# Forming sums of up-projection weight blocks earlier, in the attention, and passing them through DRAM

## The chip, the cores and the metric

One core of a Trainium2 chip runs the whole program. The metric is the device time of one execution in microseconds; several executions are timed and their median is given. One further execution was taken with the hardware profiler, and every row below is from it. PE is TensorE (matmuls), PEld its weight loads, DVE is VectorE, ACT is ScalarE, POOL is GpSimd and SP is SyncE, which issues the transfers.

## The reference

One encoder layer with shared weights runs on two batches, one of 1024 tokens (`x_prompt`) and one of 512 (`x_sample`), width 1024, all in float32. The layer is

```
h    = rmsnorm(x)
proj = h @ w_in                          # q, k, v of two attentions, and two gates
a    = dilated attention, 3 groups of 4 heads, merged by their log-sum-exp
bo   = windowed attention, 8 query heads on 2 key heads, with a sink
x    = x + (sigmoid(g_a) * (a @ w_a_out) + sigmoid(g_b) * (bo @ w_b_out)) @ w_o
u    = dwconv3(rmsnorm(x) @ w_up)        # width 2 * 2816
y    = x + (gelu(u_gate) * u_val) @ w_down
out  = rmsnorm(y)
```

The part that matters here is `rmsnorm(x) @ w_up` for the 1024 tokens.

## The kernel before, in words

Every float32 matrix is split into a rounded high part and the remainder (`hi`, `lo`), and a product is three matmuls (high by high, high by low, low by high). A weight tile is therefore loaded (`raw`), cast on ScalarE (`whi`, line 138) and its remainder formed on GpSimd, or each third time on VectorE (`wlo`, line 141). This is `wload` (lines 124 to 142). Its `raw` tiles come from one pool of three buffers of 128x1024 float32, and the `whi`, `wlo` tiles from a pool of three pairs; both pools serve all of the kernel but the 1024-token request's feed-forward part.

The order of stages is: the 512-token request as a whole, then the 1024-token request's attention, its merge of the branches, its up-projection and its down-projection.

**Attention** (lines 609 to 716). Six dilated steps (three groups, two pairs of heads each) and four steps of windowed attention follow each other. Each step has four units for the 1024 tokens, so there are 40 units, 24 of them dilated. `_Pipe.run` (lines 75 to 95) works through the units of a step: it calls the unit's score steps in turn, lets the transposes and the value products follow some steps later, and in between draws the projections of the next step (`q_pair`, `k_pair`, `v_group`) from a generator, evenly over the step. The weights of a projection are loaded when its generator starts. The v tiles of groups 1 and 2 are stored to DRAM and loaded back in another order. In this stage the compiler's tile layer orders each engine's queue by when it expects instructions to be ready, program order first among those that are.

**Up-projection of the 1024 tokens** (`up_strassen`, from line 1025). It is a Strassen-like scheme: tokens in two halves, the 1024 inputs in two halves, gate and value columns as two halves, in 22 groups of 128 gate and 128 value columns. A group needs seven products instead of eight (`m1` to `m7`, 12 matmuls each). With g0, g1 the upper and lower halves of the gate columns and v0, v1 those of the value columns, the weights of the products are g0 for m1, g1 for m2, s = v0 + v1 for m5, s - g0 for m6, g0 - v0 for m7, v1 for m4 and g1 - (s - g0) for m3. They take four GpSimd instructions of 128x512 a group: three in `sums` (from line 1053) and one when m7 is prepared. The code of `sums`, with `gp` a GpSimd instruction at line 1051:

```
gp(s, v0, v1, ALU.add)
gp(v0, g0, v0, ALU.subtract)
gp(g0, s, g0, ALU.subtract)
```

In the second line v0 becomes g0 - v0, and in the third g0 becomes s - g0; both work in place in the loaded tiles `rraw` (six buffers of 128x1024), and `s` has a pool `rsum` of three. `prepare` runs four products ahead of TensorE and splits each weight block (`ring_split`, lines 1017 to 1023: cast `rhi` on ScalarE, remainder `rlo` on VectorE) into a ring of seven. A group's gate and value columns are loaded whole at m1, 512 KB each, in pieces of 128 columns. `evacuate` adds the products together and, at m3, does the convolution, the gate and a store of the result to DRAM (line 1105).

The scheme starts while the merge still ends: the generator `quads` (lines 913 to 1004) scales and transposes the tokens (`xn`, line 950), and forms sums of token blocks (`ht`, `t2raw`, line 940; `t1lo`, line 933; `b22lo`). There an order written out by hand (`order`) interleaves its steps with the first products of three groups; up to the step "." each queue has program order.

Of the kernel before, what the change touches and what calls it, by code (L numbers as in the profile page):

```python
# [16 lines left out]
F32 = mybir.dt.float32  # L17
# [3 lines left out]
ALU = mybir.AluOpType  # L21
# [3 lines left out]
P = 128  # L25
D = 1024
KT = D // P
HD = 64
AH = 4
D_FF = 2816  # L30
FT = D_FF // P
# [33 lines left out]
class _Pipe:  # L65
# [9 lines left out]
    def run(self, units, gens, steps):  # L75
# [6 lines left out]
        for a_steps, b_steps, c_step in units:  # L82
            left = [len(b_steps)]
            base = self.t
            for need, b in b_steps:
                self.todo_b.append((base + need + 1 + self.lag_b, b, left, c_step))
# [32 lines left out]
class _Layer:  # L119
# [489 lines left out]
    def attention(self, ctx, rows=None, vectors=None):  # L609
# [39 lines left out]

        cur = {}  # L650
# [6 lines left out]
        for g in range(3):  # L657
            stats = self.sm.tile([P, NT, 2, AH], F32, tag="stats", name="stats")
            for jp in range(2):
# [25 lines left out]
                pipe.run(units, gens, steps)  # L685
# [3 lines left out]
        for pair in range(4):  # L689
# [24 lines left out]
            pipe.run(units, gens, steps)  # L714
# [197 lines left out]

    def quads(self, sm, psum, ptag):
# [111 lines left out]
    def up_strassen(self, quads):  # L1025
# [21 lines left out]
        def block(i, name, kh):  # L1047
            return groups[i][name][:, 4 * kh:4 * kh + 4].rearrange("p k c -> p (k c)")

        def gp(out, a, b, op):  # L1050
            nc.gpsimd.tensor_tensor(out=out, in0=a, in1=b, op=op)

        def sums(i):
            g0, v0, v1 = block(i, "g", 0), block(i, "v", 0), block(i, "v", 1)
            groups[i]["s"] = s = self.rsum.tile([P, 512], F32, tag="rsum", name="rsum")
            gp(s, v0, v1, ALU.add)
            gp(v0, g0, v0, ALU.subtract)
            gp(g0, s, g0, ALU.subtract)

        def prepare(i, m):  # L1060
            g = groups[i]
            blk = lambda name, kh: block(i, name, kh)
            if m == "m1":
                for name, col in (("g", i * P), ("v", D_FF + i * P)):
                    g[name] = raw = self.rraw.tile([P, KT, P], F32, tag="rraw", name="rraw")
                    nc.sync.dma_start(raw, W["w_up"][:, col:col + P].rearrange("(k p) c -> p k c", p=P))
            elif m == "m5" and "s" not in g:
                sums(i)
            elif m == "m7":
                gp(blk("g", 1), blk("g", 1), blk("g", 0), ALU.subtract)  # L1070
            src = {"m1": ("g", 0), "m2": ("g", 1), "m6": ("g", 0), "m7": ("v", 0), "m4": ("v", 1), "m3": ("g", 1)}
            g[m] = self.ring_split(g["s"] if m == "m5" else blk(*src[m]))
# [40 lines left out]
        for i in range(2):  # L1113
            prepare(*next(todo))
            sums(i)
# [299 lines left out]
```

## Time and profile before

| what | us |
|---|---|
| median of three executions | 2269.03 (2264.22 to 2269.49) |
| the profiled execution's own time | 2266.72 |
| its span, first to last instruction | 2264.9 |
| PE busy | 2178.8 |
| DVE, ACT, POOL busy | 1283.3, 1014.9, 517.4 |

The own time is what the timer gave for the profiled execution; the span is what its trace covers, 1.8 us less. Busy times of engines overlap, so they don't add up; an engine that is off the chain costs nothing by being idle. In rows, a time at the left is the start in us from the span's start, the next number is the length; in brackets stands how long the engine sat idle before and which instruction or transfer released it. A queue's issues carry a q (SPq). PEclk is the granted TensorE clock, 1.00 being its upper level.

### The profile page before, as it was taken

The page shows a single profiled execution, that of the slowest core. Times are in us where ns is not written, and L with a number is a line of the kernel's source. Part 1 is how long each engine was busy: PE and PEld are TensorE (multiplying, and loading weights), DVE is VectorE, ACT ScalarE, POOL GpSimd, SP SyncE. Part 2 cuts the span into 40 slices and gives each one's busy share as a digit, 9 for nine tenths or more (in the row PEclk, how much of TensorE's full clock was granted, in tenths as well). Part 3 has the DMA queues.
Part 4 walks back from the last instruction along what each step waited for, and adds up shares of the span by engine and source line. Part 5 has one row for each costly group of instructions (what it writes and reads, how often), then busy time and mean ns, then how long its engine had stood idle before and what let it go on. Part 6 is the DMA issues. An engine that isn't in the chain of part 4 may idle for free.

```text
span 2264.9 us, 28400 instructions
## 1 busy us (share of the span) xinstructions
PE 2178.8 (96%) x10627; PEld 1811.3 (80%) x10627; DVE 1283.3 (57%) x2191; ACT 1014.9 (45%) x1874; POOL 517.4 (23%) x296
## 2 busy tenths in 40 slices
PE   7999999899999999999999999999899999999998
PEld 6887777688878888988787788887778888888887
DVE  4547533644464456465586634325888888863534
ACT  5646532533344336565576211124555555543433
POOL 1211144233333411010000132232333333300000
PEclk9999999999999999999999899999999999999999
DMA  5453452323333331413112911113122222264452
GB/s 169 138 171 115 141 162 89 112 85 110 94 112 112 93 98 47 135 58 122 55 50 83 253 45 54 42 45 131 56 75 84 84 82 80 85 212 142 160 170 102
DMA packets 247981, 240.80 MB, mean 106 GB/s; under 512 B 19808, under 2 KB 204848, under 8 KB 247844
## 3 DMA queue, kind: packets, MB, share of 16 engines
q1 hardware_dynamic: 247844, 238.99, 33.9%
q8 instruction: 83, 1.36, 0.2%
q14 instruction: 54, 0.44, 0.1%
HBM read 202.46 MB, written 42.79 MB: 108 GB/s over the span
## 4 chain that ended last, share of the span: by engine, by line
PE 76%; DVE 6%; issue 3%; ACT 2%; DMA 1%; POOL 1%; SPq 0%; DVEq 0%; ACTq 0%; POOLq 0%
PE psuA L1015 10%; PE psuC L1015 5%; PE pacc L835 4%; PE pacc L1175 3%; PE pacc L1174 3%; PE pacc L1176 3%; PE pacc L834 3%; PE pacc L833 3%; PE psu L148 3%; PE psu L147 3%; PE psu L149 3%; PE psg L149 3%; PE psg L148 3%; PE psg L147 3%; PE psuB L1015 2%
## 5 line engine op out<-in xcount | busy, mean ns | idle before, releaser
L141 POOL TENSOR_TENSOR wlo<-raw,whi 128x1024 fp32r<-128x1024 f32 (+1 forms) x117 | 275.1, 2356 | 901.7 <-ACT whi L138 713.2
L138 ACT CAST whi<-raw 128x1024 fp32r<-128x1024 f32 (+1 forms) x178 | 182.4, 1031 | 380.5 <-PE pacc L835 134.8
L847 DVE TENSOR_TENSOR xacc<-xacc,pacc 128x512 f32<-128x512 f32 x240 | 160.5, 686 | 127.7 <-PE pacc L835 127.3
L141 DVE TENSOR_TENSOR wlo<-raw,whi 128x1024 fp32r<-128x1024 f32 (+1 forms) x61 | 75.7, 1242 | 147.1 <-ACT whi L138 147.0
L147 PE MATMUL psg<-hhi,whi 128*128 128x512 f32 x384 | 149.6, 390 | 1.2 <-ACT frow L520 1.2
L149 PE MATMUL psg<-hhi,wlo 128*128 128x512 f32 x384 | 149.4, 389 | 0.0
L148 PE MATMUL psg<-hlo,whi 128*128 128x512 f32 x384 | 149.4, 389 | 0.0
L1021 ACT CAST rhi<-rraw 128x512 fp32r<-128x512 f32 x132 | 81.4, 623 | 135.6 <-PE psuA L1015 52.3
L147 PE MATMUL psu<-hhi,whi 128*128 128x512 f32 x352 | 137.3, 391 | 0.0
L149 PE MATMUL psu<-hhi,wlo 128*128 128x512 f32 x352 | 137.2, 390 | 0.0
L148 PE MATMUL psu<-hlo,whi 128*128 128x512 f32 x352 | 137.0, 390 | 0.0
L1175 PE MATMUL pacc<-rlo,rhi 128*128 128x512 f32 x328 | 127.7, 389 | 0.0
L1176 PE MATMUL pacc<-rhi,rlo 128*128 128x512 f32 x328 | 127.6, 389 | 0.0
L1174 PE MATMUL pacc<-rhi 128*128 128x512 f32 x328 | 127.4, 389 | 0.0
L1022 DVE TENSOR_TENSOR rlo<-wraw,rhi 128x512 fp32r<-128x512 f32 x82 | 53.3, 687 | 115.6 <-ACT rhi L1021 115.6
L1022 DVE TENSOR_TENSOR rlo<-rraw,rhi 128x512 fp32r<-128x512 f32 x132 | 104.5, 818 | 23.0 <-ACT rhi L1021 21.1
L804 DVE TENSOR_TENSOR sg<-sg,psa 128x512 f32<-128x512 f32 x48 | 32.9, 687 | 140.3 <-PE psa L149 115.5
L1021 ACT CAST rhi<-wraw 128x512 fp32r<-128x512 f32 x82 | 47.1, 619 | 129.3 <-PE pacc L1176 125.6
L147 PE MATMUL psq<-hhi,whi 128*128 128x512 f32 x240 | 99.4, 414 | 1.3 <-DVE vb L356 0.7
L148 PE MATMUL psq<-hlo,whi 128*128 128x512 f32 x240 | 95.8, 399 | 0.0
L149 PE MATMUL psq<-hhi,wlo 128*128 128x512 f32 x240 | 95.4, 398 | 0.0
L414 DVE TENSOR_TENSOR ptlo<-pst,pthi 128x512 fp32r<-128x512 f32 (+1 forms) x128 | 82.6, 654 | 14.3 <-ACT pthi L413 12.8
(264 smaller groups left out, 6089.2 us busy)
## 6 DMA issues: line engine op xcount, KB each, us to landing
raw<-in_w_in_dram SPq DMA_DIRECT2D x80, 512.0 KB
raw<-in_w_up_dram SPq DMA_DIRECT2D x44, 512.0 KB
rraw<-in_w_up_dram SPq DMA_DIRECT2D x44, 512.0 KB
wraw<-in_w_down_dram SPq DMA_DIRECT2D x44, 512.0 KB
raw<-in_w_down_dram SPq DMA_DIRECT2D x22, 512.0 KB
gv<-y SPq DMA_DIRECT2D x22, 512.0 KB
graw<-gv SPq DMA_DIRECT2D x44, 256.0 KB
raw<-in_w_o_dram SPq DMA_DIRECT2D x16, 512.0 KB
```

What stands on the lines that cost most here:

```text
L138: nc.scalar.copy(out=hi[:, :n], in_=raw[:, :n])
L141: eng.tensor_tensor(out=lo[:, :n], in0=raw[:, :n], in1=hi[:, :n].bitcast(F32), op=ALU.subtract)
L147: mm(out, whi, r[0], start=start, stop=False)
L148: mm(out, whi, r[1], start=False, stop=False)
L149: mm(out, wlo, r[0], start=False, stop=stop)
L847: nc.vector.tensor_tensor(out=x, in0=x, in1=p, op=ALU.add)
L1015: mm(out, a[:, cols], b, start=start and j == 0 and n == 0, stop=j == 3 and n == 2, skip_group_check=True)
L1021: nc.scalar.copy(out=hi, in_=src)
L1022: nc.vector.tensor_tensor(out=lo, in0=src, in1=hi.bitcast(F32), op=ALU.subtract)
L1174: mm(p, a, whi, start=first, stop=False)
L1175: mm(p, a, wlo, start=False, stop=False)
L1176: mm(p, b, whi, start=False, stop=last)
```

## The change

The sums are formed in the 1024-token request's attention, one group of columns at the start of each of the first 22 units, from two tiles of the `raw` pool, and stored to a DRAM tensor `u_d` of 22 x 2 x 128 x 1024. In the up-projection GpSimd does nothing more: m5 loads the two tiles of sums (4 KB a row), m1 loads the gate columns alone, and m6 loads the lower half of the value columns, 256 KB, into the pool `rsum`.

```diff
-    def run(self, units, gens, steps):
+    def run(self, units, gens, steps, each=lambda: None):
...
             base = self.t
+            each()
...
+        if not wide:
+            self.u_d = self.dram.tile([FT, 2, P, D], F32, tag="usums", name="usums")
+        todo = iter([] if wide else range(FT))
+
+        def sums():
+            for i in todo:
+                self.up_sums(i)
+                break
...
-                pipe.run(units, gens, steps)
+                pipe.run(units, gens, steps, sums)
...
-            pipe.run(units, gens, steps)
+            pipe.run(units, gens, steps, sums)
...
+    def up_sums(self, i):
+        nc = self.nc
+        l, r = slice(0, 512), slice(512, 1024)
+        a, b = (self.wp.tile([P, D], F32, tag="raw", name="raw") for _ in range(2))
+        for t, col in ((a, i * P), (b, D_FF + i * P)):
+            nc.sync.dma_start(t.rearrange("p (k c) -> p k c", k=KT),
+                              self.w["w_up"][:, col:col + P].rearrange("(k p) c -> p k c", p=P))
+        for out, x, op, y in ((b[:, r], b[:, l], ALU.add, b[:, r]), (b[:, l], a[:, l], ALU.subtract, b[:, l]),
+                              (a[:, l], b[:, r], ALU.subtract, a[:, l]), (a[:, r], a[:, r], ALU.subtract, a[:, l])):
+            nc.gpsimd.tensor_tensor(out=out, in0=x, in1=y, op=op)
+        nc.sync.dma_start(self.u_d[i, 0], a)
+        nc.sync.dma_start(self.u_d[i, 1], b)
...
             if m == "m1":
-                for name, col in (("g", i * P), ("v", D_FF + i * P)):
-                    g[name] = raw = self.rraw.tile([P, KT, P], F32, tag="rraw", name="rraw")
-                    nc.sync.dma_start(raw, W["w_up"][:, col:col + P].rearrange("(k p) c -> p k c", p=P))
-            elif m == "m5" and "s" not in g:
-                sums(i)
-            elif m == "m7":
-                gp(blk("g", 1), blk("g", 1), blk("g", 0), ALU.subtract)
-            src = {"m1": ("g", 0), "m2": ("g", 1), "m6": ("g", 0), "m7": ("v", 0), "m4": ("v", 1), "m3": ("g", 1)}
-            g[m] = self.ring_split(g["s"] if m == "m5" else blk(*src[m]))
+                g["g"] = raw = self.rraw.tile([P, KT, P], F32, tag="rraw", name="rraw")
+                nc.sync.dma_start(raw, W["w_up"][:, i * P:(i + 1) * P].rearrange("(k p) c -> p k c", p=P))
+            elif m == "m5":
+                for n, name in ((1, "vs"), (0, "gs")):
+                    g[name] = raw = self.rraw.tile([P, KT, P], F32, tag="rraw", name="rsum")
+                    nc.sync.dma_start(rows(raw), self.u_d[i, n])
+            elif m == "m6":
+                g["v"] = raw = self.rsum.tile([P, KT // 2, P], F32, tag="rsum", name="rraw")
+                nc.sync.dma_start(raw, W["w_up"][D // 2:D, D_FF + i * P:D_FF + (i + 1) * P]
+                                  .rearrange("(k p) c -> p k c", p=P))
...
             prepare(*next(todo))
-            sums(i)
```

In `up_sums` a is the gate tile and b the value tile; b is complete after the second sum, a after the fourth.

## Rows read from the trace of the kernel before

**Rows 1.** The page: TensorE's busy time, and the chain's shares by engine.
```profile
PE 2178.8 (96%) x10627; PEld 1811.3 (80%) x10627; DVE 1283.3 (57%) x2191; ACT 1014.9 (45%) x1874; POOL 517.4 (23%) x296
...
PE 76%; DVE 6%; issue 3%; ACT 2%; DMA 1%; POOL 1%; SPq 0%; DVEq 0%; ACTq 0%; POOLq 0%
```

**Rows 2.** Windows by stage: busy us per engine (count), PEclk, DMA share, GB/s.
```profile
851.00:1109.00 258.00, 254.30 (x1580) 226.30 (x1579) 144.42 (x359) 151.74 (x371) 29.19 (x14) 1.00 0.29 87
...
1577.00:1670.00 93.00, 82.19 (x350) 66.44 (x351) 82.35 (x106) 52.70 (x87) 34.23 (x21) 0.93 0.23 75
1700.00:2000.00 300.00, 300.00 (x1325) 248.43 (x1324) 244.74 (x238) 151.05 (x222) 101.97 (x59) 1.00 0.26 82
```
The five busy columns are PE, PEld, DVE, ACT and POOL.

**Rows 3.** TensorE's waits from 1530 to 1720: total us, times, longest.
```profile
PE psuB L1015 <- DVE ug L1076: 3.0, 1, 3.0
...
PE psuA L1015 <- ACT ug L1083: 1.5, 1, 1.5
```

**Rows 4.** VectorE's timeline at the start of the up-projection.
```profile
1573.78 1.42 DVE L950 TENSOR_SCALAR xn<-xacc,rs 128x1024 f32<-128x1024 f32 x2
...
1586.38 3.45 DVE L950 TENSOR_SCALAR xn<-xacc,rs 128x1024 f32<-128x1024 f32 x2
...
1592.04 2.71 DVE L940 SCALAR_TENSOR_TENSOR ht<-pst,vecs,ht 128x512 f32<-128x512 f32 x4
...
1646.56 2.31 DVE L1099 SCALAR_TENSOR_TENSOR y<-ug,vecs,y 128x1023 f32<-128x1023 f32 x1
1648.79 1.27 DVE L1099 SCALAR_TENSOR_TENSOR y<-uv,vecs,y 128x1023 f32<-128x1023 f32 x1
```

**Rows 5.** ScalarE's timeline in the same stretch.
```profile
1590.38 2.43 ACT L966 ACTIVATE ht<-pst,vecs 128x512 f32<-128x512 f32 x4 [6.46 <-PE pst L959]
```

**Rows 6.** Windows of 5 us: columns as in rows 2.
```profile
1605.00:1610.00 5.00, 4.96 (x12) 3.93 (x13) 5.00 (x9) 4.68 (x10) 0.00 (x0) 0.50 0.00 0
```

**Rows 7.** SP's queue in the timeline, before and at the attention's start.
```profile
771.12 26.92 SPq L134 DMA_DIRECT2D raw<-in_w_in_dram  x6
802.17 7.66 SPq L363 DMA_DIRECT2D bias<-skew  x6
811.76 7.11 SPq L911 DMA_DIRECT2D out_dram<-yo  x4
834.12 23.30 SPq L134 DMA_DIRECT2D raw<-in_w_in_dram  x4
```

**Rows 8.** Timeline: a weight's cast on ScalarE, and the window keys' first matmul.
```profile
830.51 1.05 ACT L138 CAST whi<-raw 128x1024 fp32r<-128x1024 f32 x1 [1.11 <-PE psv L306]
...
832.17 1.05 ACT L138 CAST whi<-raw 128x1024 fp32r<-128x1024 f32 x1
...
1068.45 0.48 PE L147 MATMUL psk<-hhi,whi 128*128 128x512 f32 x1
```

**Rows 9.** A lone load and a lone store: SP's timeline, and windows of 1 us.
```profile
1147.17 0.38 SPq L134 DMA_DIRECT2D raw<-in_w_in_dram  x1
1150.78 0.32 SPq L707 DMA_DIRECT2D ab<-ost  x1
...
1150.00:1151.00 1.00, 1.00 (x7) 0.80 (x7) 0.95 (x3) 0.98 (x3) 0.00 (x0) 1.00 0.23 69
...
1152.00:1153.00 1.00, 0.99 (x8) 0.74 (x7) 0.54 (x3) 0.57 (x3) 0.00 (x0) 1.00 0.84 344
```

**Rows 10.** Two loads, their last bytes (window) and the sum that waited for them.
```profile
1702.64 3.29 SPq L1066 DMA_DIRECT2D rraw<-in_w_up_dram  x2
...
1709.00:1710.00 1.00, 1.00 (x6) 0.84 (x5) 1.00 (x2) 0.57 (x2) 0.00 (x0) 1.00 0.07 16
...
1710.54 1.71 POOL L1051 TENSOR_TENSOR rsum<-rraw 128x512 f32<-128x512 f32 x1 [9.97 <-DMA rraw<-in_w_up_dram]
```

**Rows 11.** Timeline: the up-projection's first loads, and the first sum.
```profile
1567.88 2.92 SPq L1066 DMA_DIRECT2D rraw<-in_w_up_dram  x3
...
1575.17 1.27 POOL L1051 TENSOR_TENSOR rsum<-rraw 128x512 f32<-128x512 f32 x1 [32.81 <-DMA rraw<-in_w_up_dram]
```

**Rows 12.** Tile raw, 800 to 1250: durations in ns, least/median/most, first and last start.
```profile
L141 POOL TENSOR_TENSOR wlo<-raw,whi x17: 2369/2397/2414, 831.7 to 1243.2; 128x1024 fp32r<-128x1024 f32 x17
```

More of the change, by code (lines that the diff above doesn't have):

```diff
@@ L1048, in block @@
             return groups[i][name][:, 4 * kh:4 * kh + 4].rearrange("p k c -> p (k c)")
[L1050 to L1058, printed above, removed]
         def prepare(i, m):
@@ L1062, in prepare @@
             blk = lambda name, kh: block(i, name, kh)
+            rows = lambda t: t.rearrange("p k c -> p (k c)")
             if m == "m1":
-                for name, col in (("g", i * P), ("v", D_FF + i * P)):
-                    g[name] = raw = self.rraw.tile([P, KT, P], F32, tag="rraw", name="rraw")
-                    nc.sync.dma_start(raw, W["w_up"][:, col:col + P].rearrange("(k p) c -> p k c", p=P))
-            elif m == "m5" and "s" not in g:
-                sums(i)
-            elif m == "m7":
-                gp(blk("g", 1), blk("g", 1), blk("g", 0), ALU.subtract)
-            src = {"m1": ("g", 0), "m2": ("g", 1), "m6": ("g", 0), "m7": ("v", 0), "m4": ("v", 1), "m3": ("g", 1)}
-            g[m] = self.ring_split(g["s"] if m == "m5" else blk(*src[m]))
+                g["g"] = raw = self.rraw.tile([P, KT, P], F32, tag="rraw", name="rraw")
[8 more added lines that the diff above has]
+                                  .rearrange("(k p) c -> p k c", p=P))
+            src = {"m1": ("g", 0), "m2": ("g", 1), "m5": ("vs", 1), "m6": ("gs", 0), "m7": ("vs", 0), "m4": ("v", 0),
+                   "m3": ("gs", 1)}
+            g[m] = self.ring_split(blk(*src[m]))
         def evacuate(i, m):
```

## Prediction

> **What bounds the kernel now.** I read the page's busy shares and chain first, then the windows stage by stage, because the change takes work out of one stage and puts it into another. TensorE is busy 96% of the span and makes 76% of the chain that ended last; GpSimd makes 1% of it [rows 1]. The reader should look for the stage in which GpSimd's sums cost TensorE anything at all. It is not the steady up-projection: there TensorE is busy 300.00 of 300 us, with GpSimd at 101.97 us [rows 2]. What is idle lies at the start of that projection: 82.19 of 93 us are busy between 1577 and 1670. The stage that takes the new work, the dilated part of the 1024-token attention (851 to 1109), has 3.7 us idle in 258, so there is nearly nothing to win there and much to lose.
>
> TensorE's own waits at the projection's start that bear on this are two of 3.0 us on VectorE and two of about 1.5 us on ScalarE, one of each kind shown [rows 3]. Behind them is a VectorE that runs slow while GpSimd sums: the same pair of scalings takes 1.42 us at 1573 and 3.45 at 1586; the same convolution step takes 2.31 us at 1646 and 1.27 at 1648 [rows 4].
>
> **What the removal gives.** In the steady projection the four sums of each group, their GpSimd time and VectorE's slow instructions go; worth nothing, since TensorE is full [rows 2]. At its start, step by step. VectorE reaches the `ht` differences at 1592.04 [rows 4], while ScalarE could read the same bank at 1590.38 [rows 5]; without the sums VectorE is idle there, so the whole VectorE chain up to both 3.0 us waits moves 1.7 us earlier, and that is all that these two give (one chain). At 1646 and twice more near it convolution steps take 2.31 us and not 1.27, 3.1 us together, more than the last two waits, so these 2.9 us go. The granted clock is 0.50, the lower level of 1.2 GHz, from 1605 to 1610, after the second 3.0 us gap [rows 6]: 2.5 us of work lost. A shorter gap may keep it or not; I take half, 1.2 us. Together 1.7 + 2.9 + 1.2 = 5.8 us, with bounds 1.7 (the first term alone) and 7.1.
>
> The loads change too: the first three groups need three loads of 512 KB instead of six before the first products. TensorE's first product also needs ScalarE's and VectorE's turns, which stay, so nothing is taken (bounds: nothing and one load, 4.5 us, of gain). The stored sums of these groups are due with the `t1` operands, which VectorE has not begun at 1592 [rows 4], over 20 us after the first loads go out (1567.88 [rows 11]); nothing again. Each later group loads 1.75 MB for 1 MB; the cover is the load's lead, a group of 19 us (84 matmuls at the pace of 1325 in 300 us [rows 2]), against some 5 us a load; were it gone, a late load of 4.5 us in 19 groups would cost 86 us.
>
> **What the addition costs.** Each of the first 22 of 40 attention units (24 are dilated) now takes two of the three `raw` buffers, loads 2 x 512 KB into them, makes four 128x512 sums on GpSimd and stores 2 x 512 KB. These are the buffers in which every projection weight lands. Two queues are passed as well: SP issues four more DMAs a unit, and behind a store that waits for its sums stand weight loads, bias loads and the reloads of v; GpSimd gets four sums a unit, and behind sums that wait for their loads stand the weights' differences. What decides is the buffers, since they set when any of these can go.
>
> Today a weight is loaded far ahead. Six loads go out from 771 to 798 and then the ring is full; the next goes at 834.12, when buffers come free [rows 7]. Its cast waits for TensorE to finish an earlier projection (830.51 and 832.17) [rows 8]. Until about 836, then, one buffer or two are held by waiting weights, and I allow the sums of one unit to be finished by then. The weight of the window keys is needed at 1068.45 [rows 8], behind 21 units' sums. Less 8.0 us for its own load, cast and difference (4.5 as below, 1.05 [rows 8], 2.4 [rows 12]), 20 units have 1060.5 - 836 = 224 us: **11.2 us each**. Slower than that and TensorE waits; what attention work its queue holds ahead of the late weight could hide a little of it, which I don't count.
>
> How long is a unit's loop on a buffer? A lone 512 KB weight load is issued at 1147.17 and its bytes end about 1150.2 (0.23 of that us is busy); a lone 512 KB store is issued at 1150.78 and its bytes end about 1152.9 [rows 9]. The signal comes later: the second of the two loads issued from 1702.64 on had its last bytes about 1709.1 (0.07 of that us), and GpSimd, waiting for it, began at 1710.54 [rows 10], 1.4 us. I add that to both (for the store no row shows it): 4.5 us a load, 3.5 us a store. A sum takes 1.27 us [rows 11], and the 128x1024 differences in the attention stay between 2369 and 2414 ns, whatever VectorE does [rows 12], so I take 1.27 there as well. The value tile needs two sums before it is stored: 4.5 + 2.5 + 3.5 = 10.5 us. The gate tile needs four: 4.5 + 5.1 + 3.5 = 13.1. Which loop decides depends on the queue's order; the tool that arranges the queues does not keep program order (the bias loads at 802.17 stand ahead of the y stores at 811.76, which the program writes earlier [rows 7]), so I expect the value tile's store to go when it is ready, and its loop to set the pace.
>
> Those are lone transfers. The stretch moves 87 GB/s at a DMA share of 0.29 now [rows 2]. Twenty-two units bring 46.1 MB in its 258 us, 179 GB/s; at the same bytes per share that is 0.60 more, 0.89 in all. At the start of the up-projection, where the loads come in a row, the first value load was issued second, about 1568.4, and its sum began at 1575.17, 6.8 us later [rows 11]; I put the share there at 1. Between 4.5 at 0.29 and 6.8 at 1 the straight line gives 6.4 at 0.89: a loop of 12.4 us, 1.2 over what there is, **24 us late** over 20 units. Bounds: nothing (10.5 us, it keeps pace) and 76 us (the gate tile's loop in traffic, 6.4 + 5.1 + 3.5 = 15.0). I take 24, since 0.89 is nearer the busy row than the lone one.
>
> [...]
>
> VectorE in the attention: nearly all its instructions there read PSUM, and those kept their 0.7 us beside GpSimd at 1592 (2.71 us for four [rows 4]); nothing is taken. Bias loads go out three heads at a time at first (six at 802.17 [rows 7], two a head) and cost nothing while SP is not stuck for longer than some 20 us.
>
> **The sum.** Own time of the profiled run 2266.7 (span 2264.9) - 5.8 + 24 = 2284.9. The median of the runs, 2269.0, stands 2.3 higher; on that footing 2287.
>
> **Rivals.** (A) The sums keep pace: loop 10.5 under 11.2, weights arrive in time, only the start's gain is left: 2266.7 - 5.8 + 2.3 = 2263. It decides at a loop of 11.2 us. For it: lone transfers are that short. Against it: the traffic that the sums bring themselves. [...] (B) The gate tile's store ends the loop: 13.1 us lone gives 38 us late, 2301; 15.0 in traffic gives 76, 2339. For it: program order puts the gate store first. Against it: the reordering seen. (C) Both small: the loop just fits and the start gives little, 2266 to 2275; it also covers sums that gain nothing because VectorE's work, not GpSimd, sets the start.
>
> **How the numbers follow.** Forecast 0.42 (2273 to 2303), A 0.28, B 0.16, C 0.14. A change of 0.3%, 6.8 us, is about what a measurement of this kernel tells from none. A at 2263 sits at that edge: I give faster 0.25; same 0.17, from the rest of A and most of C; slower 0.58. The range goes from 2257 (A with the 7.1 us bound and the 4.5 us of an earlier first load) to 2320, which holds the forecast, A, C and the lower half of B. The forecast's own range is 2273 to 2303.
>
> **What would show it.** Right: GpSimd's sums among the attention's groups at about 1.3 us each; waits of SP's loads for a store's landing; TensorE's idle time between 851 and 1109 grown from 3.7 to some 25 us, put down to a weight's cast or difference; DMA share near 0.9; the scaling pair at 1586 back to 1.4 us and the two convolution waits gone; the steady projection still full. Wrong: TensorE's idle time in the attention unchanged (A), idle gaps in the steady projection (late loads), or a start that keeps its four waits.

## The result, and the profile after

The changed kernel takes **2336.74 us** (median of 4 runs, 2335.86 to 2343.74) against 2269.26 us before (4 runs, 2264.22 to 2269.83): a ratio of 1.0314, 95% interval 1.0293 to 1.0335. It is 67 us slower, where 18 were forecast. The profiled run took 2343.74 us, its span is 2342.0 us; against the span before, 2264.9, that is 77.1 us. The accounts below are made between these two spans.

From the first products of each stage in the two traces: the attention's last value product begins at 1230.0 before and at 1312.3 after, 82.3 us later; from there to the up-projection's first product it takes 347.9 and 347.7 us; from that to the up-projection's last product 441.1 and 435.8, a gain of 5.3; the rest takes 245.9 and 246.2. So 82.3 - 0.2 - 5.3 + 0.3 = 77.1. The loss lies ahead of the attention's end. The attention's first product comes 6.8 us later too (808.58 and 815.37), but that is not the change's: TensorE's last long gap ahead of the attention, 6.75 us in both, ends at 426.89 before and at 433.19 after, long ahead of the first sum; and the run of the addition alone starts its attention at 807.29, a control without sums at 814.48. Without these 6.8 us the profiled run loses 70.3, near the 67 of the medians. The rest of the 82.3, 75.5 us, is the attention itself.

The page after, the lines of [rows 1], and the new group of sums in the list of the costliest groups (busy us, mean ns of one, idle time before them):

```profile
PE 2205.8 (94%) x10627; PEld 1833.3 (78%) x10627; DVE 1222.0 (52%) x2191; ACT 1013.1 (43%) x1874; POOL 481.0 (21%) x296
...
PE 46%; DMA 5%; POOL 3%; issue 2%; ACT 2%; DVE 2%; SPq 0%; POOLq 0%; DVEq 0%; ACTq 0%
...
L933 POOL TENSOR_TENSOR raw<-raw 128x512 f32<-128x512 f32 x88 | 116.7, 1327 | 144.1 <-DMA raw<-in_w_up_dram 126.0
```

The chain has passed in part from TensorE to transfers and GpSimd. The windows that answer to [rows 2], the two of the up-projection at later times, since it starts 82 us later:

```profile
851.00:1109.00 258.00, 211.16 (x1226) 186.69 (x1224) 111.20 (x258) 111.99 (x263) 119.25 (x86) 0.92 0.65 211
...
1660.00:1753.00 93.00, 86.73 (x378) 70.74 (x379) 73.64 (x109) 53.92 (x89) 0.00 (x0) 0.95 0.41 138
1750.00:2050.00 300.00, 300.00 (x1325) 248.51 (x1324) 190.82 (x233) 148.92 (x219) 0.00 (x0) 1.00 0.38 124
```

In these 258 us of the attention TensorE is idle for 46.8 us, not 3.7, and has done 1226 products, not 1580. The steady projection is full, as before. At its start 6.3 us are idle and not 10.8. The DMA share of the attention is 0.65; the prediction had worked out 0.89.

The attention as a whole, from its first product to the start of the last, and its part from the window keys' first product on; of each the first row is before and the second after:

```profile
808.58:1230.00 421.42, 409.49 (x2527) 356.58 (x2528) 257.87 (x651) 253.88 (x618) 39.54 (x22) 1.00 0.24 76
815.37:1312.30 496.93, 431.32 (x2527) 373.22 (x2528) 258.88 (x651) 253.00 (x618) 150.90 (x108) 0.95 0.49 157
...
1068.45:1230.00 161.55, 151.04 (x882) 123.44 (x881) 118.42 (x303) 111.84 (x281) 9.58 (x4) 1.00 0.15 48
1132.15:1312.30 180.15, 167.06 (x962) 137.39 (x961) 125.94 (x325) 121.34 (x305) 13.61 (x7) 0.99 0.22 68
```

The products are the same 2527. TensorE is idle for 65.6 us of the attention and not 11.9, 53.7 more, and is busy 21.8 us longer with the same products, at a mean granted clock of 0.95 and not 1.00. These two make the 75.5.

In the chain of waits, the stretch from 962 to 980 shows one round of the sums and the next one's load, with nothing between (start, us, what):

```profile
962.09 4.89 DMA raw<-in_w_up_dram
...
967.12 1.26 POOL raw L933
...
968.45 1.27 POOL raw L933
...
969.79 1.28 POOL raw L933
...
971.14 1.29 POOL raw L933
...
972.45 2.66 DMA usums<-raw
...
975.12 4.54 DMA raw<-in_w_up_dram
```

From load to load it is 975.12 - 962.09 = **13.0 us**: a load, all four sums, and the landing of the store that follows the fourth. The order on SP says why it is the fourth and not the second sum. SP's queue in the timeline (the value tile's store is L935, the gate tile's L934, the next loads L929, gate first):

```profile
853.64 0.34 SPq L935 DMA_DIRECT2D usums<-raw  x1
856.38 0.34 SPq L934 DMA_DIRECT2D usums<-raw  x1
...
929.20 0.32 SPq L935 DMA_DIRECT2D usums<-raw  x1
931.94 0.32 SPq L934 DMA_DIRECT2D usums<-raw  x1
932.45 1.02 SPq L929 DMA_DIRECT2D raw<-in_w_up_dram  x1
...
935.02 0.38 SPq L929 DMA_DIRECT2D raw<-in_w_up_dram  x1
...
1119.08 0.32 SPq L934 DMA_DIRECT2D usums<-raw  x1
1119.74 0.38 SPq L135 DMA_DIRECT2D raw<-in_w_in_dram  x1
```

The value tile does go out first, at 929.20. But the buffer that it frees is taken by the next set's first load, which is the gate tile. The value tile, which the first sum needs, gets the buffer that the gate tile's store frees, at 935.02. The second set's last store goes out at 856.38 and the 21st's at 1119.08: 19 sets in 262.7 us, **13.83 us a set**, where a unit of the attention takes 258 / 24 = 10.75 us before.

Who waits, from 800 to 1160 (total us, times, longest), on SP, ScalarE and TensorE:

```profile
SPq L935 <- POOL raw L933: 56.9, 21, 3.8
SPq L934 <- POOL raw L933: 51.0, 21, 4.2
SPq L935 <- DMA raw<-in_w_up_dram: 47.5, 19, 4.7
```
```profile
ACT vs L312 <- DMA v<-vs: 67.8, 14, 17.7
ACT whi L139 <- DMA raw<-in_w_in_dram: 41.1, 9, 6.5
```
```profile
PE psv L305 <- DVE vs L313: 34.8, 9, 12.2
```

SP stands still for 155 us before the sums' stores. Behind it wait weights, and the stores of v, whose single staging buffer (`vs`) ScalarE needs again: that wait is 67.8 us now, and in the kernel before, in the same window, it was 6.8:

```profile
ACT vs L311 <- DMA v<-vs: 6.8, 3, 2.7
```

TensorE's longest wait in the attention, 12.24 us, is of this kind. In order: a sum's store on SP, the store of v behind it (L315), ScalarE's next copy into `vs`, and the product that needs the bank which the copy empties:

```profile
957.10 0.32 SPq L935 DMA_DIRECT2D usums<-raw  x1
...
963.30 2.08 SPq L315 DMA_DIRECT2D v<-vs  x1
...
969.27 0.37 ACT L312 CAST vs<-psv 128x256 fp32r<-128x256 f32 x1 [17.75 <-DMA v<-vs]
...
970.15 0.58 PE L305 MATMUL psv<-whi,hhi 128*128 128x256 f32 x1 [12.24 <-DVE vs L313]
```

The next longest, 9.5 us up to 1087.50, ends behind such a copy as well. No wait of TensorE between 800 and 1160 is put down to a weight's cast or difference.

### The profile page after: what moved, and what is told of

It reads as the page before. It is cut to its first block, busy times and chain, and to the rows that moved or that the text cites. A ratio compares the mean times of both kernels' runs of the same rounds, so it can differ in the third digit from the quotient of the medians.

```text
span 2342.0 us, 28629 instructions
## 1 busy us (share of the span) xinstructions
PE 2205.8 (94%) x10627; PEld 1833.3 (78%) x10627; DVE 1222.0 (52%) x2191; ACT 1013.1 (43%) x1874; POOL 481.0 (21%) x296
## 3 DMA queue, kind: packets, MB, share of 16 engines
q8 instruction: 83, 1.36, 0.2%
## 4 chain that ended last, share of the span: by engine, by line
PE 46%; DMA 5%; POOL 3%; issue 2%; ACT 2%; DVE 2%; SPq 0%; POOLq 0%; DVEq 0%; ACTq 0%
PE psuA L1039 10%; PE psuC L1039 5%; PE pacc L1193 3%; PE pacc L1192 3%; PE pacc L1194 3%; POOL raw L933 3%; PE psuB L1039 2%; DMA raw<-in_w_up_dram 2%; PE psg L148 2%; PE psg L149 2%; PE psg L150 2%; DMA raw<-in_w_in_dram 1%; DMA usums<-raw 1%; PE pacc L844 1%; PE pacc L843 1%
## 5 line engine op out<-in xcount | busy, mean ns | idle before, releaser
L933 POOL TENSOR_TENSOR raw<-raw 128x512 f32<-128x512 f32 x88 | 116.7, 1327 | 144.1 <-DMA raw<-in_w_up_dram 126.0
L305 PE MATMUL psv<-whi,hhi 128*128 128x256 f32 x288 | 89.9, 313 | 42.2 <-DVE vs L313 35.6
L1045 ACT CAST rhi<-rsum 128x512 fp32r<-128x512 f32 x88 | 54.5, 622 | 115.9 <-PE psuC L1039 65.7
L305 PEld LDWEIGHTS psv<-whi,hhi 128*128 128x128 f32 x288 | 61.5, 214 | 45.1 <-DVE vs L313 29.8
```

What stands on the lines that cost most here:

```text
L305: mm(ps[:, :256], hi, whi, start=k == 0, stop=False)
L933: nc.gpsimd.tensor_tensor(out=out, in0=x, in1=y, op=op)
```

## The experiments

Times are single runs beside one of the kernel before on the same chip (2261 to 2270 us), unless an interval is given. "Set" is one call of `up_sums`, "period" the mean time between the last stores of sets 2 and 21.

**The addition alone.** The attention of after, with the up-projection of before; the stored sums are not used.

```diff
-                for n, name in ((1, "vs"), (0, "gs")):
-                    g[name] = raw = self.rraw.tile([P, KT, P], F32, tag="rraw", name="rsum")
-                    nc.sync.dma_start(rows(raw), self.u_d[i, n])
...
+            elif m == "m5" and "s" not in g:
+                sums(i)
```

> The attention of the changed kernel with the up-projection of the kernel before: sums are formed and stored, and not used. Every theory of what slows the attention expects it as slow as in the changed kernel, 497 us from the first v projection to the last value product (421 before). It tells the two parts apart: if the up-projection gives back 5 us as the traces show, this run is about 5 us slower than the changed kernel, 2342 (2337 + 5); if the up-projection gives nothing, 2337.

Measured 2334.83, before 2261.3. The attention takes 493.8 us, 72 more than before. All of the loss is in the addition; nothing of it comes from the up-projection's new loads. As a time it is under both forecasts; over its own kernel before it is 73.5 us, where the change is 67.5 over its own. That fits a gain of 5 in the up-projection, but a single run doesn't show it.

**What in the set costs.** Without the sums:

```diff
-        for out, x, op, y in ((b[:, r], b[:, l], ALU.add, b[:, r]), (b[:, l], a[:, l], ALU.subtract, b[:, l]),
-                              (a[:, l], b[:, r], ALU.subtract, a[:, l]), (a[:, r], a[:, r], ALU.subtract, a[:, l])):
-            nc.gpsimd.tensor_tensor(out=out, in0=x, in1=y, op=op)
```


> The changed kernel without the four GpSimd sums of each unit (the loaded tiles are stored as they are, so the up-projection works on other weights): same buffers, same transfers, same queue entries on SP. Buffer theory (a unit holds two of the three raw buffers for load, four sums and store; the loop is 5.0 + 5.3 + 3.0 = 13.3 us where 11.2 are to be had): the loop falls to 5.0 + 3.0 = 8 us, the attention to about 425 us, the run to about 2265. SP-queue theory: waits for the sums fall away too, most of the loss goes, 2265 to 2285. Traffic theory: the same bytes move, so it stays near 2337 or gets worse. GpSimd theory: about 2265.

Measured 2285.24. Period 11.87 us, attention 444.4. The window of the attention:

```profile
851.00:1109.00 258.00, 241.99 (x1471) 214.11 (x1470) 135.01 (x332) 139.81 (x340) 24.50 (x12) 0.97 0.71 229
```

With all transfers and more traffic per us (229 GB/s for 211), 52.6 of the attention's 75.6 us are back. So the bytes by themselves are not the main cause: the sums' 5.35 us in the round are. A round of load and store alone is some 7.6 us, and the period of 11.87 is then near the unit's own 10.75. The time is at the upper end of what the queue theory gave (2265 to 2285) and 20 us above the buffer theory's 2265.

Loading the tile that is needed first, first:

```diff
-        for t, col in ((a, i * P), (b, D_FF + i * P)):
+        for t, col in ((b, D_FF + i * P), (a, i * P)):
```


> The changed kernel with the value tile loaded first, so that it takes the buffer that comes free first and the gate tile, needed one sum later, the one that the gate tile's store frees. Buffer theory: the loop loses one sum, 13.3 to 12.0 us, 21 times 1.3, some 25 us less than the changed kernel, about 2310. Other theories: no change, 2337.

Measured 2318.18: one exchanged pair of loads gives back 18.6 us, less than the 25 of the buffer theory and well clear of the others' nothing. Period 12.83, attention 476.9. This takes one sum (1.36 us from start to start) out of the round; the period falls by 1.00, and the time follows: 22 x (13.83 - 12.83) = 22.

Half the work: one tile, two sums, and the same tile stored twice.

```diff
-        a, b = (self.wp.tile([P, D], F32, tag="raw", name="raw") for _ in range(2))
...
+        b = self.wp.tile([P, D], F32, tag="raw", name="raw")
...
+        for out, x, op, y in ((b[:, r], b[:, l], ALU.add, b[:, r]), (b[:, l], b[:, r], ALU.subtract, b[:, l])):
...
-        nc.sync.dma_start(self.u_d[i, 0], a)
+        nc.sync.dma_start(self.u_d[i, 0], b)
```


> Only the value tile is loaded, two of the four sums are made, and the tile is stored twice, so that the up-projection works on other numbers: one buffer for two, three transfers of 512 KB for four. In the runs so far with one set of sums a unit, the attention took 22 times the sums' loop plus 177 to 199 us (loops of 11.9 to 16.3 us). Pace theory (a unit can't be shorter than the loop, and has 10.75 us of its own work): load 5, sums 2.6 and store 3 make 10.6, so nothing or little is lost: 2263 to 2280. Load theory (each transfer and sum costs its share): half to three quarters of the loss stays, 2297 to 2320.

Measured 2303.95, a miss for the pace theory, which had a threshold in it. The period is 12.96 us and not 10.6. SP's queue shows the difference:

```profile
905.67 0.32 SPq L932 DMA_DIRECT2D usums<-raw  x1
...
917.56 0.34 SPq L932 DMA_DIRECT2D usums<-raw  x1
...
928.16 0.34 SPq L932 DMA_DIRECT2D usums<-raw  x1
```

One round is 10.6 us, but the one before it, with a weight's load between (issued at 909.55), is 11.9, and there are some with stores and reloads of v between. The attention's own entries in the queue are part of the round; the sum of a set's own steps is only its least length. So the loss has no sharp threshold, and the rival's numbers (2297 to 2320) held.

**Which resource.** Stores issued by GpSimd, so that SP never stands behind a sum:

```diff
-        nc.sync.dma_start(self.u_d[i, 0], a)
-        nc.sync.dma_start(self.u_d[i, 1], b)
+        nc.gpsimd.dma_start(self.u_d[i, 0], a)
+        nc.gpsimd.dma_start(self.u_d[i, 1], b)
```


> The changed kernel with the two stores of a unit issued by GpSimd and not by SP, so that no load on SP stands behind a store that waits for sums. SP-queue theory: the weights no longer wait behind the stores, most of the 76 us in the attention go, 2275 or less. Buffer theory: the buffers are held as long as before, the attention stays at 480 to 500 us, 2325 to 2340. Traffic theory and GpSimd theory: no change or a little worse.

Measured 2354.86, period 14.70: the queue theory's 2275 or less falls, the time is 15 us above the buffer theory's range, and a little worse than the change, as the traffic and GpSimd theories had it. SP now waits in another place, at the next loads, for the buffer, as its waits from 800 to 1160 show:

```profile
SPq L929 <- DMA usums<-raw: 96.9, 23, 12.2
```

One buffer for two, each set in two halves with sums of 128x256, and the same with GpSimd's stores (the edit just shown):

```diff
+        for q in range(2):
+            both = self.wp.tile([P, D], F32, tag="raw", name="raw")
+            a, b = both[:, 0:512], both[:, 512:1024]
...
```


> The changed kernel with each unit's work done in two halves, each half in one raw buffer (half of the gate rows and half of the value rows, 2 x 256 KB), so a step never needs two buffers at once: same bytes, same sum elements on GpSimd (eight 128x256 instructions for four 128x512), more queue entries on SP (eight loads and four stores a unit). Buffer theory: a half holds one buffer for some 4.5 + 2.8 + 3 = 10 us, two halves run side by side in the three buffers, so a unit needs about 10 us of two buffers or 7 of three, under the 11.2: the attention falls to 425 to 440 us, the run to 2263 to 2280. SP-queue, traffic and GpSimd theories: nothing that they count gets less, 2330 or more.

> The halves of e4 (one raw buffer a half) with their stores issued by GpSimd. e4 was slower because SP went one half at a time: a store waiting for its sums held the next half's load behind it. Buffer theory with SP as second constraint: with both taken away two halves overlap, the attention falls below 440 us, the run to 2265 to 2290. If e4's loss came from something else (shorter transfers, the GpSimd instructions, traffic), it stays above 2330.

Measured 2366.87 and 2378.23: the buffer theory misses by 87 and 88 us, and the rivals' 2330 or more holds. The halves did not overlap; in the chain the loads, four sums of 0.74 us and the stores follow each other, one half after the other, with periods of 15.49 and 16.25 us. In the first of the two a half's store, issued at 935.43 as its sums end, stands ahead of the next half's load at 936.00: a second buffer that is free is of no use behind a queue that is in order.

The weights' buffers themselves were untested still, so the sums got two of their own. The room comes from three other pools of the attention, and a control has the smaller pools and no sums:

```diff
-        self.bp = pool("bp", 4 if wide else 3)
-        self.qk = pool("qk", 16 if wide else 10)
+        self.bp = pool("bp", 4 if wide else 2)
+        self.qk = pool("qk", 16 if wide else 9)
...
-        self.sm = pool("sm", 2)
+        self.sm = pool("sm", 2 if wide else 1)
+        self.us = None if wide else pool("us", 2)
...
-        a, b = (self.wp.tile([P, D], F32, tag="raw", name="raw") for _ in range(2))
+        a, b = (self.us.tile([P, D], F32, tag="usum", name="usum") for _ in range(2))
```


> The kernel before with less room in the 1024-token attention: nine head buffers for ten, two bias buffers for three, one stats buffer for two; no sums there. It is the control for the two runs with buffers of their own. Every theory: it says what the lost room costs by itself, 2265 to 2285 us.

> The change with two buffers of its own for the sums, so that the three weight buffers are no longer shared; the room is that of the control. Buffer theory (load, sums and store hold buffers that weights need): weights come in time again, and what is left is the traffic, at most the 23 us of the run without sums: the control's time and up to 25 us more. Queue theory (weight, bias and v loads stand in SP's queue behind stores that wait for sums, some 110 to 170 us of waits): the loss stays, the control and 50 us or more.

The control took 2276.79, the sums with their own buffers **2354.7**: 78 more, as the queue theory had it (50 or more). So the theory that I had held until then, that the loss comes from sharing the weights' buffers, falls. The weights' casts no longer wait for their loads, but TensorE waits as long, from 800 to 1345:

```profile
PE psv L305 <- DVE vs L313: 33.3, 4, 18.8
PE psv L306 <- POOL wlo L142: 30.1, 2, 24.2
```

The first is the store of v in SP's queue again, the second a weight's difference that stands behind sums in GpSimd's queue. With all four DMAs of the sums on GpSimd as well, nothing of them is left in SP's queue or in the weights' buffers:

```diff
-            nc.sync.dma_start(t.rearrange("p (k c) -> p k c", k=KT),
+            nc.gpsimd.dma_start(t.rearrange("p (k c) -> p k c", k=KT),
...
-        nc.sync.dma_start(self.u_d[i, 0], a)
-        nc.sync.dma_start(self.u_d[i, 1], b)
+        nc.gpsimd.dma_start(self.u_d[i, 0], a)
+        nc.gpsimd.dma_start(self.u_d[i, 1], b)
```

> Own buffers for the sums as in the run that took 2355, and all four of their DMAs issued by GpSimd, so that nothing of the sums is left in SP's queue or in the weight buffers; 22 units in a row. Queue theory: the control (2277) and up to 30 us, what is left being the weights' differences that stand behind sums in GpSimd's queue and the traffic. If the traffic itself slows v's stores and the weights: 2320 or more.

Measured 2398.51, the slowest of all. Period 16.21; GpSimd's queue is now the one that holds the others up. TensorE waits for a weight's difference, and SP, with nothing of the sums in it, for the buffers that these differences free (800 to 1345; the like wait before was 118.5):

```profile
PE psv L306 <- POOL wlo L142: 47.2, 2, 30.9
...
SPq L135 <- POOL wlo L142: 283.8, 16, 43.3
```

The time lies where the other side had put it ("2320 or more", from traffic). That traffic is the cause isn't shown: the DMA share from 851 to 1109 is 0.54 here, and 0.65 in the change.

**Fewer sets at a time.** The 22 sets over all 40 units:

```diff
-        todo = iter([] if wide else range(FT))
+        turns = iter([] if wide else range(40))
...
-            for i in todo:
-                self.up_sums(i)
+            for n in turns:
+                for i in range(n * FT // 40, (n + 1) * FT // 40):
+                    self.up_sums(i)
                 break
```


> The changed kernel with the same 22 sums spread over all 40 units of the attention (22 in 40) in place of the first 22. Buffer theory: a unit of sums needs 13.3 to 14 us of the ring and now has some 17, so the weights come in time nearly everywhere: attention 421 to 435 us, run 2264 to 2280. Traffic theory: the share falls from 0.64 to about 0.5, a third of the loss stays, 2285 or more.

Measured 2318.45 (4 runs; ratio 1.0221, 1.0204 to 1.0238), a miss for the buffer theory: only 18 us come back, and the traffic theory's 2285 or more holds. But the run without sums moves the same bytes in a shorter attention and loses less, so the bytes alone don't explain it. The same edit with the buffers of their own:

> Own buffers and spread sums together, stores on SP. If buffers and pace together make the loss: within 10 us of the control. If SP's queue makes it: about the control and 40 us.

Measured 2358.9, 82 us over the control and above both forecasts, but this run says nothing on spreading: the sets were not spread. The period is 14.78, with 84 instructions of GpSimd from 851 to 1109 where the run without spreading has 85. Probably, with no weights' buffer to tie them down, the sets are put ahead by whatever arranges the queues; that isn't shown.

The spreading and GpSimd's stores, two edits shown above, together:

> The spread sums (22 over 40 units) with GpSimd issuing the stores, so that SP never waits for a sum. With SP issuing them the spread kernel took 2318. If what the spreading leaves is SP's queue: 2280 to 2290. If it is the shared buffers or the traffic: 2310 to 2325.

Measured 2337.22, worse than SP's and above both forecasts. Then the v stores on ScalarE's queue, in the changed kernel and in the spread one:

```diff
-                nc.sync.dma_start(self.v_d[g - 1, kt * P:(kt + 1) * P, :],
+                nc.scalar.dma_start(self.v_d[g - 1, kt * P:(kt + 1) * P, :],
```


> The change with one line of before moved to another queue: ScalarE, and no longer SP, issues the 16 stores of v in the two later groups of heads. Queue theory (a v store stands in SP's queue behind loads that wait for a buffer and stores that wait for sums; ScalarE's next v copy waits for it, 67.8 us in the changed kernel and 6.8 before): those waits fall to some 15 us and the time to 2290 to 2315, since the weights still come late. Buffer theory (only the weights decide): 2325 to 2340.

> Both together: 22 sums over 40 units, where weights wait only 3 us for their loads, and the v stores on ScalarE's queue. Queue theory: the 40.6 us of v waits go and 2270 to 2295 is left (2318 with the spreading alone). Traffic or buffer theory: 2305 to 2320.

Measured 2345.57 and 2306.94, both above what the queue theory gave; the first is above the rival's range too, and the second lies in it (2305 to 2320). In the first ScalarE's wait for the v stores is halved:

```profile
ACT whi L139 <- DMA raw<-in_w_in_dram: 43.3, 7, 8.6
ACT vs L312 <- DMA v<-vs: 34.7, 11, 7.2
```

and nothing is gained. TensorE's wait behind `vs` falls from 34.8 to 14.9 us, and its waits for two other casts of ScalarE grow to 16.3 and 14.0, from 8.2 and 6.1. So the stores of v are where the loss showed and not what made it; it fits a round that sets the pace whoever waits for it. In the second, which has room between the sets, it gives 11.5 us, about a fifth of what the spreading had left. TensorE's longest wait is then one of 16.5 us in the window part, and SP's queue shows the statistics that start it going out right behind a sum's store, as late as 1138.55:

```profile
1138.12 0.34 SPq L935 DMA_DIRECT2D usums<-raw  x1
1138.55 2.12 SPq L500 DMA_DIRECT2D stat<-stats  x4
```

These and their reloads (L529), moved to ScalarE too, and a control with the same moves and no sums:

```diff
-            nc.sync.dma_start(bass.AP(tensor=dst.tensor, offset=base + off, ap=ap + e), src)
+            nc.scalar.dma_start(bass.AP(tensor=dst.tensor, offset=base + off, ap=ap + e), src)
...
-            nc.sync.dma_start(st[:, g], self.stat_d[g].rearrange("(b p) e -> p b e", p=P))
+            nc.scalar.dma_start(st[:, g], self.stat_d[g].rearrange("(b p) e -> p b e", p=P))
```

> The spread sums with v's stores, and now also the stores and reloads of the softmax statistics, on ScalarE's queue. In the run before (2307) the statistics were ready at about 1125 and went out at 1138.5, behind a sum's store in SP's queue; TensorE then waited 16.5 us for a window unit. Queue theory: these 16.5 us go and the time is 2282 to 2296. Any theory in which the sums' traffic or GpSimd's time makes the loss: 2300 to 2310.

> Its control: the kernel before with the same three kinds of DMA on ScalarE's queue and no sums in the attention. Every theory: within 8 us of before, 2262 to 2278; what it differs by is the price of the other queue.

The control took 2263.8 against 2266.72, so the other queue costs nothing by itself. But the spread kernel took 2318.18, 11 us more than without the move and above both forecasts. The 16.5 us wait is gone, but TensorE has three others from 1100 to 1290 (total us, times, longest):

```profile
PE pso L425 <- DVE ptlo L415: 11.2, 4, 9.4
PE pss L403 <- DVE q L263: 10.0, 1, 10.0
PE psvt L352 <- ACT vt L348: 8.9, 1, 8.9
```

Emptying SP's queue customer by customer moves the loss about.

**As few as help.** Only the first six groups' sums go through DRAM, one set in every sixth unit; the other sixteen stay on GpSimd in the up-projection.

```diff
-            for i in todo:
-                self.up_sums(i)
+            for n in turns:
+                if n % 6 == 4 and n // 6 < EARLY:
+                    self.up_sums(n // 6)
                 break
```


> Sums through DRAM for the first six groups only, formed in every sixth unit of the attention; the other 16 groups form theirs on GpSimd in place, as before. If the gain of 5.3 us in the up-projection is all at its start (the steady part is full either way) and six units of sums fit beside the weights, the run is 4 to 6 us faster than before, 0.2%; if the gain needs all groups, it is no faster than before.

Measured 2265.79 (11 runs) against 2266.92 (15 runs): a ratio of 1.000, 0.9989 to 1.001. In its trace the up-projection gains the 5.3 us in full (435.8) and the attention loses 3.4 (424.8). No difference can be measured.

**The runs together.** All with one set in every unit:

| run | period, us | attention, us | attention less 22 periods |
|---|---|---|---|
| no sums | 11.87 | 444.4 | 183 |
| value tile first | 12.83 | 476.9 | 195 |
| half the work | 12.96 | 463.4 | 178 |
| the addition alone | 13.77 | 493.8 | 191 |
| **the change** | 13.83 | 497.0 | 193 |
| v stores on ScalarE | 14.20 | 504.2 | 192 |
| own buffers | 14.57 | 511.8 | 191 |
| stores by GpSimd | 14.70 | 515.3 | 192 |
| halves | 15.49 | 522.8 | 182 |
| own buffers, all by GpSimd | 16.21 | 555.9 | 199 |
| halves, stores by GpSimd | 16.25 | 534.6 | 177 |

Before, 22 units of 10.75 us are 236.5 of the attention's 421.4, which leaves 185. The last column stays near that, between 177 and 199, in all eleven: what is lost is lost while the sets run, and their period accounts for it. This places the loss. That the round causes the period, and not the other way, is shown by the run with the value tile first, and by the chain from 962 to 984, which has nothing but the round in it. It isn't so throughout: from 860 to 1140 the round's loads, sums and stores make 18.9, 22.3 and 9.6% of the chain, and half of it passes through weights' loads and the attention's own work.

## Why the prediction was wrong

**The direction and the place were right**: the loss is in the 1024-token attention, and the rest is near the forecast. **The size was wrong**: 24 us were forecast for the addition; the attention is 75.6 us longer (421.4 before, 497.0 after). Of these 53.7 are idle time of TensorE, where the prediction had 24, and 21.8 are the same products at a lower granted clock, for which it had nothing in this stage.

The step that failed is "so I expect the value tile's store to go when it is ready, and its loop to set the pace". The first half is right. The second does not follow: a set is two loads, and the one that its first sum waits for is issued second, into the buffer that the gate tile's store frees. The round is that of the pair: load 4.89, sums 5.35 and store 2.66 in the round above, 13.0, and 13.83 a set with what stands between; 12.4 was taken. In length that is rival B, "the gate tile's store ends the loop", which was given 0.16. Its lone value, 13.1, is what the round measures, not 15.0: the lone prices of 4.5 and 3.5 stayed about right (the ten whole loads in the chain from 860 to 1140 take 3.8 to 6.9 us, seven of them under 5.1; landings of stores 2.6 to 3.4), and the slowing by traffic that was to make every load 6.4 us did not come, at a DMA share of 0.65 for the 0.89 worked out. That B's 2339, its price in traffic, lies 2 us from the measured 2336.74 is luck: a round of 15.0 was not there, and the clock that makes up for it was not in its sum.

With 13.83 in the prediction's own formula, 20 units end at 836 + 277 = 1113, and the window keys' weight is ready 8.0 us on, at 1121, 52 us late. The keys' first product in the trace:

```profile
1132.15 0.48 PE L148 MATMUL psk<-hhi,whi 128*128 128x512 f32 x1
```

The weight is loaded right behind the 21st set's last store (at 1119.74), as the prediction said, and its difference is done at 1128.3, 7 us after the formula's time; 6.8 of these are the late start of this profiled run. But the keys' first product, 63.7 us later than in [rows 8], did not stand waiting for it: TensorE's longest wait between 1100 and 1132 is 1.9 us. TensorE had stood still before, longest behind the copies into `vs`, 34.8 us in nine waits. So the second step that failed is the victim: the signs of being right were to be waits "put down to a weight's cast or difference", and there are none. That 52 is near the 53.7 us of added idle time is therefore no proof of the path. From the keys on the attention takes 18.6 us more than before; 16.0 of them are busy time, since 80 of the products that came ahead of the keys before come behind them now, and 2.6 are idle. It was also said that "what decides is the buffers". They make the round, but the run with buffers of their own shows that taking them out doesn't help, since SP's and GpSimd's in-order queues tie the attention's steps to the sets as well. The prediction named both queues and priced neither, and the store of v, for which ScalarE waits longest (67.8 us), stands in none of its steps; it names the reloads of v alone.

The other steps:
- **Steady projection, nothing**: right, 300.00 of 300 us.
- **Start of the up-projection, 5.8**: 5.3 measured, with a different make-up. The scaling pair is back to 1.42 us, and the convolution steps to 1.28, as said. Of the two 3.0 us waits on VectorE, expected to give 1.7 together, one gave 0.8 and the other 0.1; the two on ScalarE (2.9) are gone. That leaves 1.5, which I put down to the clock; the window that answers to [rows 6] shows the better granted clock, 0.66 for 0.50, in the last of these rows:

```profile
PE psuA L1039 <- ACT rhi L1045: 3.1, 1, 3.1
PE psuC L1039 <- DVE b22lo L964: 2.9, 1, 2.9
PE psuB L1039 <- DVE ug L1095: 2.2, 1, 2.2
```
```profile
1685.00:1690.00 5.00, 3.59 (x9) 2.87 (x10) 5.00 (x9) 4.37 (x10) 0.00 (x0) 0.66 0.00 0
```

VectorE reaches the `ht` differences 0.7 us behind ScalarE and not 1.66 [rows 4, 5], so the chain could move by 0.9 only: it ran into ScalarE.
- **Loads of later groups, hidden**: right; the projection has no gap.
- **Sums of 1.27 us in the attention**: right, 1.33 in the mean of 88.

For the transfers that GpSimd issued a rule can be compared. In the run with all four DMAs of a set on GpSimd a store of 512 KB landed 2.9 us after its issue in the median, and a load of 512 KB, in pieces of 512 bytes, 5.1 us. The Trainium skill fits a DMA that GpSimd issues as 2.0 us and its bytes at 436 GB/s ("DMA: Bandwidth & Descriptors", Anatomy of one DMA); by that estimate 512 KB take 3.2 us. The stores are near it, the loads are longer.

What stays open: no kernel had its sums in own buffers, on a queue that nothing else uses, and with the weights' differences off GpSimd, so it isn't shown that the loss ends when all three ties are cut. Nor is it settled what each 10 us wait of the spread kernels comes from. What the traffic and the added entries in SP's queue cost by themselves is bounded by the run without sums: its attention is 23 us longer than before, and ScalarE's waits for the stores of v are part of it.

## What to carry to other kernels

Work "for an idle engine" that is loaded, computed and stored through shared in-order queues has a round time, from load to load on the same buffer, and that time is to be compared with the unit of work beside it before anything else; work out the round from the tile that the first step needs, at the place in the queue where its load really stands. Here, with a round longer than the unit, moving entries to other queues or adding buffers mostly shifted the wait; a shorter round, or fewer sets, is what helped. And ask how many of the sets bring the gain: here six of 22 gave all of the 5.3 us.

## What was not expected of the hardware

- **The granted clock fell with the gaps.** In the attention's window, with TensorE busy 211 of 258 us, it was 0.92 in the mean of its two levels (2.4 and 1.2 GHz), where [rows 2] has 1.00; from 900 to 1000 in the run with own buffers, where TensorE was busy 57 of 100 us, it was 0.78. Over the whole attention the same 2527 products were busy 431.32 us at a mean of 0.95, and 409.49 at 1.00: 21.8 us of the loss are not idle time. The prediction charged the clock at the projection's start and not here.
- **Traffic slowed transfers little.** At 211 GB/s seven of the ten whole 512 KB loads in the chain took under 5.1 us, against the 4.5 that the prediction worked out for a lone one.
- **A DMA issued by GpSimd takes its time from the engine**: 0.59 us for a store and 0.91 for a load in the run with all four on GpSimd, where the fourth sum begins at 939.74, as the 0.58 us of a store's issue from 939.13 on end. The period was longer in each of the four kernels with GpSimd's stores than in its partner with SP's (14.70 for 13.83, 16.25 for 15.49, 16.21 for 14.57, and with the spreading 18.62 for 17.85).
